# Two mixing layers of a one-core transformer block: the planner's priorities come from a written list of stage steps

## The chip, the cores and the metric

The kernel runs on one core of a Trainium2 chip. The core's engines each take their own instruction queue in order: TensorE (PE, matmuls and transposes), VectorE (DVE), ScalarE (ACT), GpSimd (POOL), and SyncE (SP), which issues the DMAs. They wait for each other by semaphores. The metric is the device time of one launch in microseconds (us); lower is better. The kernel before takes 1844.59 us, the median of three runs (1842.2 to 1846.6).

## The reference, cut to what matters

A block with two layers (DEPTH = 2) runs over 512 latent tokens and 256 context tokens of width 1024, in float32. Each layer is a mixing sublayer followed by an MLP; in the second layer the context is only read, so it has no outputs there. The mixing sublayer splits one projection of the input into four groups:

```
def mixing_sublayer(h_ctx, h_lat, pos, ctx_out, w_in, w_out, ...):
    (a, cq, ckv, kpe, q, k, v, rq, rk, rv, gf, gb) = split_cols(h @ w_in)   # context and latent
    ya = conformer_conv(a)              # a * sigmoid, 31-tap depthwise convolution, layer norm, silu, matmul
    yb = mla(cq, ckv, kpe)              # 4 heads, low-rank q and kv, rope, softmax attention
    yc = gqa(q, k, v)                   # 4 query heads, 2 kv heads, normed, rope, softmax attention
    yd = retention(rq, rk, rv, gf, gb)  # 4 heads, forward and backward, chunks of 128, gated readout
    return concatenate([ya, yb, yc, yd]) @ w_out
for layer in range(DEPTH):
    x = x + g1 * mixing(modulate(x, sh1, sc1))
    x = x + g2 * relu(modulate(x, sh2, sc2) @ w1) ** 2 @ w2     # the context too, in layer 0
return rms_norm(x, final_g)
```

`conformer_conv`, `mla` and the rest are independent of each other until the last matmul. The shifts, scales and gates come from small matmuls of the conditioning vectors with `w_mod`.

## The kernel before, in words

Most matmuls are done in a split form: a float32 operand becomes a high and a low part (`split`: a cast on DVE or ACT, then a subtraction on DVE or POOL), and `mm3` issues three matmuls per product. So each weight tile that arrives by DMA costs work on DVE, ACT or POOL before PE can use it, and so does each intermediate result.

The kernel's Python code does not issue instructions directly. Each call on an engine is recorded (`Plan.record`) with its data dependencies, its place in the record as its priority, and the engines that may do it; copies, splits and elementwise products may often go to one of two or three. `Plan.schedule` then replays the record with a cost table: whenever an engine is free it takes the available operation of lowest priority number, and the order found this way is issued on each engine. The order is thus fixed at build time; at run time nothing is reordered. All of it is issued from one helper line (L645), so rows of the trace carry that line and must be told apart by their tiles and shapes: taps read `cvw`, gains of the grouped-query attention are `gg`, PSUM tiles are `b` and `pp`, and everything else in SBUF is `m`. `Plan` also keeps a model of what DVE and POOL may not do at the same time (`_port`) and of ACT's function tables (a switch to another of `Exp`, `Silu`, `Sigmoid` is charged).

In `mixing` every stage is a generator, and `go(k, n)` advances stage `k` by up to `n` steps, which is when its operations are recorded. The stages are:

- `um`, `ug`, `ur`: projections for the MLA, the grouped-query and the retention group, on PE, one token tile per step; `a`: the convolution's input with its sigmoid gate; `gates`: the retention gates, with silu.
- `mla`, `gqa`: norms, rope and splits of the projected queries and keys, mostly on DVE, ACT and POOL; one token pair per step.
- `taps`: the convolution, 31 steps of two DVE instructions (one per channel half), 62 in all, each 783 columns wide in layer 0 and 512 in layer 1.
- `ln`: layer norm, silu and the pointwise matmul behind the convolution, one token pair per step; needs all taps.
- `u`: attention units, 24 in layer 0 and 16 in layer 1 (the first half MLA, the second half grouped-query). A unit is scores on PE, a minimum on DVE, exp on ACT, a scaling, transposes on PE, splits, a second matmul.
- `rin`, `ret`, `read`: retention set-up, its four heads, and its readout.
- `todo`: in layer 0 six pieces of modulation for later layers.

`out_proj` follows; its matmuls read the four groups in the order convolution, MLA, grouped-query, retention. The order of the steps comes from `order_of(l, nu)`, built from the tables `o0`, `o1`, `Q` and `TP`. Written out, it is this:

```
0: um mla a taps ug gqa ur todo:0 u:1 gates ln u:1 (x10) todo:1 u:1 (x3) todo:4 todo:5 u:1 u:1 todo:2
   rin todo:3 then (u:1 ret:1) x7, u:1, u ret read
1: um mla a taps ug gqa ur u:1 ln gates u:1 (x10) rin then (u:1 ret:1) x5, u ret read
```

A name without a number means all steps that are left, `u:1` means one.

Of the kernel before, what the change touches and what calls it, by code (L numbers as in the profile page):

```python
# [20 lines left out]
MC = 184  # L21
F = (0, 0)
R = (15, 3)
Q = (1, 1)
EARLY = 0
XO = 0
XL = 0
# [4 lines left out]
RSV = 88  # L32
TL = 0
TM = (0, 0, 0)
TP = (7, 20, 25, 26, 23, 23)
REL = 160.0
LONG = 300
FB = 100
# [6 lines left out]
nraw = 3  # L45
nmd = 2
nw = 10
o0 = (1, 0, 0, 9)
o1 = (1, 1, 0, 6)
J = (0, 7)  # L50
D_ = (3, 3)
NCUT = 2

DM = 1024
DFF = 4096
# [613 lines left out]
        return self.cx[hl][j]  # L669


def order_of(l, nu):

    g, x, ln, r = (o0, o1)[l][:4]
    seq = [(k, 1000) for k in ("um", "mla", "a", "taps", "ug", "gqa", "ur")] + [("u", g)]
    if x:
        seq += [("ln", 1000), ("gates", 1000)]
        at = -1
    else:
        seq += [("gates", 1000)]  # L680
        at = max(ln, g)
    if at == g:
        seq.append(("ln", 1000))
    for i in range(g, nu):
        seq.append(("u", 1))
        if i + 1 == at:
            seq.append(("ln", 1000))
        if i == nu - r:
            seq.append(("rin", 1))
        if i > nu - r and Q[l] and (i - nu + r) % Q[l] == 0:  # L690
            seq.append(("ret", 1))
    seq += [(k, 1000) for k in ("u", "ret", "read")]
    if l == 0:
        for j in sorted(range(6), key=lambda j: (-TP[j], -j)):
            seq.insert(min(TP[j], len(seq) - 2), ("todo", j))
    return seq


@with_exitstack
def block_kernel(ctx: ExitStack, tc: tile.TileContext, x, c, cx, c_ctx, w_mod, b_mod, w_in, w_out,  # L700
# [37 lines left out]
    def psG(shape=(128, 512), nm="psG"):  # L738
        return plan.tile(ph, "g", shape, F32, nm)
# [157 lines left out]
    def acc_cols(l, i, conds):  # L897
        accs = mod_acc(l, i, conds)
        for cond in conds:
            for n in range(2):  # L900
                p = psT((128, 4, 128))
                for ft in range(4):
                    a = (n * 4 + ft) * 128
                    T.transpose(p[:, ft], accs[cond][:, a:a + 128], ident)
                V.tensor_reduce(out=modc[l][:, MI[i], cond, n * 4:n * 4 + 4], in_=p, axis=AX.X, op=ALU.add)
            if i in (1, 4):
                G.tensor_scalar(out=modc[l][:, MI[i], cond], in0=modc[l][:, MI[i], cond], scalar1=1.0, scalar2=1.0,
                                op0=ALU.add, op1=ALU.mult)

    def acc_gate(l, i, conds, res):  # L910
        accs = mod_acc(l, i, conds)
        for cond in conds:
            res[cond] = wkt([128, DM], nm="gate")
            ah, al = (wkt([128, DM], F32R, nm="mhl") for _ in range(2))
            split(ah, al, accs[cond])
            for n in range(2):
                p = psT()
                for k, a in enumerate((al, ah)):
                    T.matmul(p, lhsT=ones.bitcast(F32R), rhs=a[:, n * 512:(n + 1) * 512], start=k == 0, stop=k == 1)
                VS.copy(out=res[cond][:, n * 512:(n + 1) * 512], in_=p)  # L920
# [87 lines left out]
    def mixing(l, ht, yt, todo, late=None):  # L1008
# [153 lines left out]
        um, ug, ur, vg, gates, mq, mk, mvv = {}, {}, {}, {}, {}, {}, {}, {}  # L1162
# [192 lines left out]
        units = []  # L1355
# [235 lines left out]
        def s_read():  # L1591
            for pr in opairs:
# [18 lines left out]
                for kk in range(2):  # L1611
                    for i in range(2):
# [5 lines left out]
                                        gates=s_gates, ln=s_ln, u=s_units, ret=s_ret, read=s_read).items()}  # L1618

        def go(k, n=1000):  # L1620
            if k == "rin":
                return ret_in()
            if k == "todo":
                plan.lag = TL
                todo[n]()
                plan.lag = 0
                return
            for _ in range(n):
                if next(gens[k], self_) is self_:
                    break  # L1630

        self_ = object()
        for k, n in order_of(l, len(units)):
            go(k, n)


# [17 lines left out]
    def mlp(l, ht, tiles, xs, gate, segs, then=None):  # L1654
        NCH = DFF // 512

        def first(ch):
            hid = []
            for f in range(4):
# [3 lines left out]
                for s in segs:  # L1663
                    n = (512, 256)[s]
                    o = psG(nm="h")
                    cut = (0, 256, 512) if l == DEPTH - 1 and ch == 0 and f < NCUT else (0, n)
                    for a, b in zip(cut, cut[1:]):
# [85 lines left out]
    def later(i, n):  # L1753
# [7 lines left out]
        else:  # L1761
            mod_cols(0, i, n * 512, 512, (mod_rows, mod_rows32)[how])
    
    mixing(0, ht, yt, [lambda i=i, n=n: later(i, n) for i in (3, 4, 2) for n in range(2)],
           begin)
    xt = {t: load_x(t) for t in CTX + LAT}
    out_proj(0, yt, CTX + LAT, xt, gate)
    ht = ActT(bigt, True)
    for pr in PAIRS:
# [4 lines left out]
    todo = [lambda: acc_cols(1, 0, (0, 1)), lambda: acc_cols(1, 1, (0, 1)), lambda: acc_cols(1, 3, (0,)),  # L1774
            lambda: acc_cols(1, 4, (0,)), lambda: acc_gate(1, 2, (0,), gate1)]
# [7 lines left out]
    xt = {t: xt[t] for t in LAT}  # L1783
    yt = ActT(bigt, False)
    mixing(1, ht, yt, [])
    out_proj(1, yt, LAT, xt, gate1)
    ht = ActT(bigt, False)
# [115 lines left out]
```

## Time and profile before

| what | value |
|---|---|
| runs of the kernel before | 1844.59, 1846.6, 1842.2 us; median 1844.59 |
| the profiled execution | 1847.59 us, span 1845.9 us |
| PE busy | 1706.8 us, 92% |
| DVE busy | 1355.0 us, 73% |
| ACT busy | 684.3 us, 37% |
| POOL busy | 394.6 us, 21% |
| PE's granted clock, mean | 0.958 of full speed |

The profiled execution lasts 1847.59 us, 1.7 us more than its span, and 3.0 us more than the median of the runs. Busy shares are means over very different stages: the MLPs are matmuls in a row, while in the mixing layers (33 to 543 us and 1102 to 1476 us) PE, DVE and ACT hand small pieces to each other. A clock of 1.00 in a row is PE's 2.4 GHz, 0.50 is 1.2 GHz, and a value between is a mean over a stretch that had both.

### The profile page before, as it was taken

To read this page: it belongs to the slowest core of one execution; us is meant where nothing else is said; L and a number is where in the kernel's file an instruction comes from. 1 tells how busy PE (TensorE), PEld (TensorE's weight loads), DVE (VectorE), ACT (ScalarE), POOL (GpSimd) and SP (SyncE) were. 2 spreads that over 40 slices of the span, in tenths; PEclk is the share of its full clock that TensorE was granted. 3 is DMA by queue.
4 is the path that set the end of the run, shared out by engine and by line. 5 is a ranking of instruction groups with operands and counts; after the bars stand their busy time and mean duration, and the time that the engine had idled before them with its cause. 6 is when DMAs were issued, how large, how long until landed. Compare 5 with 4: busy or idle time off the path is not lost. (4 is left out here: it accounts for less than half of the span.)

```text
span 1845.9 us, 23213 instructions
## 1 busy us (share of the span) xinstructions
PE 1706.8 (92%) x8587; PEld 1403.2 (76%) x8587; DVE 1355.0 (73%) x2309; ACT 684.3 (37%) x1257; POOL 394.6 (21%) x358
## 2 busy tenths in 40 slices
PE   6995789989999999999999999959897989999998
PEld 4784568656788877888888889748765878888886
DVE  6889448888896788676765577974988776666665
ACT  5522027977443112111211135213997342222222
POOL 3318013651510010100100021120433421000001
PEclk9998799989999999999999999969997999999999
DMA  9220031534241434424421212110121533333331
GB/s 304 67 75 12 0 97 49 173 111 133 69 138 46 137 99 130 133 88 146 158 70 47 86 36 75 47 52 12 34 60 61 167 95 100 110 96 92 103 91 58
DMA packets 140641, 168.67 MB, mean 91 GB/s; under 512 B 7658, under 2 KB 93274, under 8 KB 140528
## 3 DMA queue, kind: packets, MB, share of 16 engines
q1 hardware_dynamic: 140528, 167.20, 29.5%
q8 instruction: 67, 1.10, 0.2%
q14 instruction: 46, 0.38, 0.1%
HBM read 161.14 MB, written 2.10 MB: 88 GB/s over the span
## 5 line engine op out<-in xcount | busy, mean ns | idle before, releaser
L645 PE MATMUL b<-m,m 128*128 128x512 f32 (+5 forms) x6452 | 1366.8, 370 | 49.6 <-DVE m L645 40.7
L645 PEld LDWEIGHTS b<-m,m 128*128 128x128 f32 (+2 forms) x6452 | 1123.2, 191 | 263.4 <-DVE m L645 39.4
L645 DVE TENSOR_TENSOR m<-m,m 128x512 fp32r<-128x512 f32 (+8 forms) x665 | 548.9, 844 | 138.0 <-PE b L645 79.9
L645 ACT CAST m<-m 128x1024 fp32r<-128x1024 f32 (+6 forms) x354 | 278.8, 808 | 666.2 <-PE b L645 462.8
L645 POOL TENSOR_TENSOR m<-m,m 128x1024 fp32r<-128x1024 f32 (+11 forms) x158 | 274.7, 1750 | 1087.7 <-ACT m L645 571.4
L645 DVE TENSOR_TENSOR m<-b,m 128x512 f32<-128x512 f32 (+12 forms) x346 | 208.6, 611 | 124.3 <-PE b L645 108.6
L645 PE MATMUL pp<-m,m 128*128 128x512 f32 (+6 forms) x848 | 206.0, 369 | 18.9 <-DVE m L645 9.7
L645 PEld LDWEIGHTS pp<-m,m 128*128 128x128 f32 (+2 forms) x848 | 148.1, 197 | 56.0 <-ACT m L645 15.8
L645 PE MATMUL b<-ident,m 128*128 128x128 f32 (+4 forms) x730 | 111.2, 280 | 27.5 <-DVE m L645 24.0
L645 ACT COPY m<-b 128x512 f32<-128x512 f32 (+7 forms) x176 | 82.8, 491 | 126.6 <-PE b L645 120.4
L645 DVE TENSOR_TENSOR m<-m 128x256 f32<-128x256 f32 (+1 forms) x104 | 63.4, 611 | 82.9 <-ACT m L645 82.4
L645 PEld LDWEIGHTS b<-ident,m 128*128 128x128 f32 (+4 forms) x730 | 84.7, 141 | 48.7 <-DVE m L645 28.2
L645 DVE SCALAR_TENSOR_TENSOR m<-m,sf,m 128x1024 f32<-128x1024 f32 x80 | 102.9, 1298 | 24.3 <-DMA m<-in_w_mod_dram 24.2
L645 DVE CAST m<-m 128x512 fp32r<-128x512 f32 (+4 forms) x163 | 77.8, 481 | 56.3 <-PE pp L645 31.7
L645 ACT ACTIVATE m<-b 128x512 f32<-128x512 f32 (+1 forms) x115 | 60.6, 529 | 149.0 <-PE b L645 140.6
L645 DVE SCALAR_TENSOR_TENSOR m<-m,cvw,m 128x783 f32<-128x783 f32 (+1 forms) x120 | 100.7, 887 | 0.6
L645 DVE TENSOR_REDUCE ty<-pp 128x1 f32<-128x768 f32 (+1 forms) x66 | 60.8, 932 | 9.2 <-PE pp L645 8.6
L645 ACT ACTIVATE m<-m 128x1024 f32<-128x1024 f32 (+4 forms) x65 | 42.0, 650 | 52.5 <-DVE m L645 42.9
L645 ACT ACTIVATE m<-pp,ty 128x768 f32<-128x768 f32 (+1 forms) x66 | 58.5, 888 | 4.4 <-PE b L645 3.0
L645 POOL TENSOR_TENSOR ty<-ty,mhalf 128x1 f32<-128x1 f32 (+4 forms) x47 | 57.3, 1225 | 2.3
L645 PE MATMUL pp<-ident,m 128*128 128x128 f32 (+3 forms) x252 | 41.6, 287 | 13.4 <-ACT m L645 7.5
L645 POOL TENSOR_SCALAR ty<-ty 128x2 f32<-128x2 f32 (+4 forms) x43 | 16.3, 380 | 166.3 <-ACT m L645 107.3
(112 smaller groups left out, 669.4 us busy)
## 6 DMA issues: line engine op xcount, KB each, us to landing
m<-in_mlp_w_dram SPq DMA_DIRECT2D x128, 512.0 KB
m<-in_w_mod_dram SPq DMA_DIRECT2D x96, 512.0 KB
m<-in_w_in_dram SPq DMA_DIRECT2D x32, 512.0 KB
m<-in_w_out_dram SPq DMA_DIRECT2D x16, 512.0 KB
m<-in_x_dram SPq DMA_DIRECT2D x8, 512.0 KB
m<-in_dist_dram SPq DMA_DIRECT2D x16, 256.0 KB
m<-in_w_in_dram SPq DMA_DIRECT2D x8, 416.0 KB
m<-m SPq DMA_DIRECT2D x24, 96.0 KB
```

The costliest lines, as they stand in the source:

```text
L645: op.fn(*[f(a) for a in op.args], **{k: f(a) for k, a in op.kw.items()})
```

## The change

`order_of` and its tables are replaced by a list per layer, read from left to right; a name with `:n` advances that stage by `n` steps, without it by all that are left. What each stage computes is not touched, and neither are the planner's rules.

```diff
-o0 = (1, 0, 0, 9)
-o1 = (1, 1, 0, 6)
+ORDER = (
+    "um mla ug gqa a ur taps:2 u:1 todo:0 gates u:2 taps:2 u:1 taps:4 u:1 taps:2 todo:1 u:2 taps:2 u:1 "
+    "taps:2 u:2 todo:4 todo:5 taps:2 todo:2 taps:2 todo:3 u:1 taps:2 u:1 taps:2 u:1 taps:2 u:1 taps:2 u:2 "
+    "taps:2 rin taps:2 u:1 taps ret:1 u:1 ln:2 ret:1 u:1 ret:1 u:1 ln ret u read ",
+    "um mla ug gqa a ur:2 u:1 taps:2 ur:2 u:1 ur taps:4 u:1 taps:2 u:1 taps:2 u:2 gates taps:2 rin ret:1 "
+    "u:3 taps:4 u:1 taps:2 u:2 ret:1 u:1 taps:4 u:1 ret:1 taps:2 u:1 taps:2 u:1 taps:2 ret u taps ln read ",
+)
...
-def order_of(l, nu):
...
+def order_of(l):
+    for w in ORDER[l].split():
+        k, _, n = w.partition(":")
+        yield k, int(n or 1000)
...
-        for k, n in order_of(l, len(units)):
+        for k, n in order_of(l):
             go(k, n)
```

In both layers `taps` leaves its place ahead of `ug` and `gqa` and is cut into pieces of two or four steps; `ug` and `gqa` come before `a`; `ln` goes from before the attention units to among the last ones in layer 0 and behind all of them in layer 1; in layer 1 `gates` moves behind the sixth unit.

**VectorE, layer 0, where the convolution runs.** Tiles: `m_3622` and `m_3628` are the convolution's inputs, `cvw` its weights; `ty` and `gg` belong to `gqa`; a 128x1024 TENSOR_TENSOR is the low part of a weight tile. Before, these rows follow 36 taps in a row:

```order
L645 SCALAR_TENSOR_TENSOR m_4837<-m_3628,cvw_163,m_4837 128x783
L645 TENSOR_REDUCE ty_3566<-m_4861 128x6 x2
L645 TENSOR_REDUCE ty_3565<-m_4929 128x6
L645 TENSOR_REDUCE ty_3565<-m_5001 128x6
L645 TENSOR_REDUCE ty_3569<-m_5001 128x6
L645 TENSOR_REDUCE ty_3569<-m_5040 128x6
L645 TENSOR_TENSOR m_5061<-b_3587,m_5011 96x512
L645 TENSOR_TENSOR m_5044<-b_3585,m_5044 96x256
L645 TENSOR_TENSOR m_5044<-b_3588,m_5044 96x256
L645 SCALAR_TENSOR_TENSOR m_4837<-m_3628,cvw_163,m_4837 128x783
L645 TENSOR_TENSOR m_4856<-m_4856,ty_3568 128x384
L645 SCALAR_TENSOR_TENSOR m_4837<-m_3628,cvw_163,m_4837 128x783
```

Now all of `gqa` stands ahead of the first tap, and the taps begin between the last two products of `a`:

```order
L650 TENSOR_SCALAR m_5020<-m_3622,cvw_163,pcol_166 128x783
L650 CAST m_5026<-m_4993 128x1024
L650 SCALAR_TENSOR_TENSOR m_5020<-m_3622,cvw_163,m_5020 128x783 x8
L650 TENSOR_TENSOR m_3628<-b_3586,m_4898 128x512
L650 SCALAR_TENSOR_TENSOR m_5020<-m_3622,cvw_163,m_5020 128x783 x2
L650 TENSOR_TENSOR m_5111<-m_4993,m_5026 128x1024
L650 SCALAR_TENSOR_TENSOR m_5020<-m_3622,cvw_163,m_5020 128x783
L650 TENSOR_TENSOR m_3628<-b_3587,m_4898 128x256
L650 SCALAR_TENSOR_TENSOR m_5020<-m_3622,cvw_163,m_5020 128x783 x19
L650 TENSOR_SCALAR m_5289<-m_3628,cvw_163,pcol_166 128x783
L650 SCALAR_TENSOR_TENSOR m_5289<-m_3628,cvw_163,m_5289 128x783
L650 TENSOR_TENSOR m_5302<-m_5022,m_5099 128x1024
```

The low parts of the weights of `ur` (`m_5111` is one) stand before or between the first twelve taps instead of behind all of `taps` and `gqa`; a run of 21 taps follows, and 58 of the 62 stand ahead of the last row of `gates`.

**ScalarE, layer 0, the silu of `ln`.** `pcol` marks the silu of `ln`, `pp` and `ty` an exp of an attention unit, `lgam` an exp of retention. Before, one table load serves the silu of `gates` and `ln` together:

```order
L645 CAST m_5413<-b_3585 128x512
L645 ACT_TABLE_LOAD
L645 ACTIVATE m_4929<-b_3588,pcol_166 128x256 x2
L645 CAST m_5448<-m_4929 128x512
L645 CAST m_5459<-m_5430 128x1024
L645 CAST m_5044<-b_3588 96x256
L645 CAST m_5477<-m_5445 128x1024
L645 CAST m_5491<-m_5465 128x1024
L645 ACTIVATE m_5522<-b_3587 128x512
```

Now each token pair's silu stands among exps, between two loads:

```order
L650 ACTIVATE m_6999<-m_6999,lgam 128x512 x2
L650 ACT_TABLE_LOAD
L650 ACTIVATE m_6765<-b_3587,pcol_166 128x256 x2
L650 ACT_TABLE_LOAD
L650 ACTIVATE m_7086,ty_3565<-pp_7030,ty_3582 128x768
L650 CAST m_7104<-b_3585 128x512
```

This pattern stands three times in layer 0; the whole program has 19 table loads instead of 10.

**GpSimd, layer 0, beside the taps.** Before, these rows of `gqa` (`m_4865`, low parts of the values) stand beside the taps, behind a weight of `ug`:

```order
L645 TENSOR_TENSOR m_4699<-m_4512,m_4658 128x1024
L645 TENSOR_TENSOR m_4865<-m_4856,m_4865 128x2x64 x2
L645 TENSOR_TENSOR m_4865<-m_4925,m_4865 128x2x64
L645 TENSOR_SCALAR ty_3567<-ty_3566 128x12
L645 TENSOR_TENSOR m_4865<-m_4925,m_4865 128x2x64
```

Now they stand before `a`'s weights, and beside the taps stands `m_5135`, the low part of the fourth and last weight piece of `ur`:

```order
L650 TENSOR_TENSOR m_4760<-m_4746,m_4760 128x2x64
L650 TENSOR_TENSOR ty_3573<-ty_3572,mhalf 128x12
L650 TENSOR_TENSOR m_4967<-m_4848,m_4875 128x1024
L650 TENSOR_TENSOR m_5135<-m_5006,m_5035 128x1024
L650 TENSOR_TENSOR m_5645<-m_5588,m_5613 128x1024
```

PE reads `m_5135` in the 19th matmul of `ur`; the row after it belongs to `todo:1` and stands behind nearly all taps.

## Rows read from the trace of the kernel before

**Rows 1.** The page's forty slices of the span: TensorE's busy share in tenths.
```profile
PE   6995789989999999999999999959897989999998
```

**Rows 2.** By stretch: us, PE, PEld, DVE, ACT, POOL busy (x), clock, DMA.
```profile
161.90:204.80 42.90, 9.04 (x28) 7.16 (x28) 40.88 (x117) 5.52 (x13) 21.58 (x18) 0.56 0.05 12
204.80:285.00 80.20, 74.53 (x338) 58.74 (x337) 23.21 (x33) 17.11 (x27) 4.63 (x5) 0.98 0.18 56
285.00:477.00 192.00, 180.57 (x1029) 127.95 (x1028) 168.23 (x349) 158.73 (x332) 89.90 (x76) 0.95 0.39 120
477.00:543.00 66.00, 65.93 (x302) 54.33 (x301) 58.38 (x77) 16.78 (x25) 18.75 (x20) 1.00 0.30 88
1195.60:1228.80 33.20, 10.53 (x33) 8.26 (x34) 32.15 (x111) 5.92 (x11) 13.80 (x18) 0.54 0.06 15
1228.80:1285.00 56.20, 56.20 (x276) 48.08 (x275) 17.39 (x25) 14.54 (x23) 0.00 (x0) 1.00 0.14 44
1285.00:1434.00 149.00, 125.77 (x722) 98.30 (x721) 134.06 (x273) 128.47 (x263) 56.33 (x52) 0.92 0.18 57
1434.00:1476.00 42.00, 42.00 (x192) 34.75 (x191) 31.78 (x43) 12.80 (x18) 19.52 (x16) 1.00 0.50 152
```

**Rows 3.** Timeline of PE, layer 0: start, us, operation, [idle before, released by].
```profile
169.10 1.62 PE L645 MATMUL b<-m 96*128 96x256 f32 x6 [7.20 <-DVE m L645]
...
185.27 1.33 PE L645 MATMUL b<-ident,m 128*128 128x128 f32 x5 [14.34 <-DVE m L645]
...
199.35 2.90 PE L645 MATMUL b<-m,m 128*128 128x512 f32 x6 [12.32 <-DVE m L645]
```

**Rows 4.** Waits of PE, 1194 to 1230 us: us in total, times, longest.
```profile
PE pp L645 <- ACT m L645: 10.3, 2, 5.4
PE b L645 <- DVE m L645: 8.7, 2, 7.9
PE pp L645 <- DVE m L645: 3.7, 1, 3.7
```

**Rows 5.** By stretch, VectorE's taps alone (`cvw`): us, busy (x), clock, DMA.
```profile
101.00:161.90 60.90, 45.93 (x47) 1.00 0.12 38
161.90:204.80 42.90, 15.70 (x16) 0.56 0.05 12
1148.00:1195.60 47.60, 36.22 (x52) 1.00 0.18 51
1195.60:1228.80 33.20, 8.11 (x12) 0.54 0.06 15
```

**Rows 6.** VectorE's groups by form, 161.9 to 199.4 us: busy us, mean ns.
```profile
L645 DVE TENSOR_TENSOR m<-m,r 128x32 f32<-128x32 f32 x48 | 5.5, 182 | 0.0
...
L645 DVE TENSOR_TENSOR m<-m,gg 128x128 f32<-128x128 f32 x6 | 1.7, 284 | 0.0
```

**Rows 7.** VectorE's groups by form, 1195.6 to 1228.8 us.
```profile
L645 DVE TENSOR_TENSOR m<-m,r 128x32 f32<-128x32 f32 x48 | 5.4, 181 | 0.0
...
L645 DVE TENSOR_TENSOR m<-m,ty 128x128 f32<-128x128 f32 x1 | 0.3, 282 | 0.0
```

**Rows 8.** Table loads of ScalarE, whole span, from the groups.
```profile
L645 ACT ACT_TABLE_LOAD x10 | 12.8, 1283 | 11.3 <-DVE ty L645 8.2 <-DMA crow<-in_c_ctx_dram 2.6 <-DVE m L645 0.3
```

**Rows 9.** Timeline, layer 1, a token pair of `ln` among `gates`.
```profile
1257.42 1.04 PE L645 MATMUL b<-ident,m 128*128 128x128 f32 x8
...
1261.93 3.06 PE L645 MATMUL b<-m,m 128*128 128x256 f32 x24
...
1264.20 0.69 DVE L645 TENSOR_TENSOR m<-b,m 128x512 fp32r<-128x512 f32 x1 [0.59 <-ACT m L645]
```

**Rows 10.** Timeline of POOL, layer 0, beside the taps and just behind them.
```profile
135.28 31.12 POOL L645 TENSOR_TENSOR m<-m,m 128x128 fp32r<-128x128 f32 x3 [20.18 <-ACT m L645]
...
166.78 0.45 POOL L645 TENSOR_TENSOR m<-m,m 128x128 fp32r<-128x128 f32 x1
```

**Rows 11.** Timeline of DVE, the same stretch.
```profile
131.17 34.10 DVE L645 SCALAR_TENSOR_TENSOR m<-m,cvw,m 128x783 f32<-128x783 f32 x36
```

More of the change, by code (lines that the diff above doesn't have):

```diff
@@ L23 @@
 R = (15, 3)
-Q = (1, 1)
 EARLY = 0
@@ L34 @@
 TM = (0, 0, 0)
-TP = (7, 20, 25, 26, 23, 23)
 REL = 160.0
@@ L669, in pair @@
         return self.cx[hl][j]
-def order_of(l, nu):
[L674 to L696, printed above, removed]
+def order_of(l):
+    for w in ORDER[l].split():
+        k, _, n = w.partition(":")
+        yield k, int(n or 1000)
 @with_exitstack
```

## The prediction

> **What bounds the kernel now.** I read the page's slices first, then the busy time by stretch, then TensorE's timeline and waits where it idles, and last the groups of VectorE there. The slices show TensorE at 9 or 8 tenths in most slices; lowest, but for the start, are the fourth (138 to 185 us, 5; the fifth has 7) and the 27th (1200 to 1246 us, 5), one in each mixing layer [rows 1]. By stretch the first is 161.9 to 204.8 us, where TensorE is busy 9.04 of 42.90 us and VectorE 40.88; the second is 1195.6 to 1228.8 us, with 10.53 of 33.20 us against 32.15 [rows 2]. In layer 0 three waits, 7.20, 14.34 and 12.32 us, make the idle time, each ended by VectorE [rows 3]. In layer 1 there are 22.7 us of waits, ended by VectorE and, through exps that waited for VectorE's minima, by ScalarE [rows 4]. What VectorE does there is the rest of the taps and then the grouped-query preparation, and only behind these come the low parts of the weights that TensorE needs for `ur`. So the bound of both places is the order of VectorE's queue. Right behind them the roles turn round: in 204.8 to 285 us TensorE runs `ur` and `gates` with VectorE busy 23.21 of 80.20 us, and in 1228.8 to 1285 us with 17.39 of 56.20 [rows 2]. Then come the attention stretches (285 to 477 and 1285 to 1434 us), where VectorE is busy 87.6% (168.23 of 192) and 90.0% (134.06 of 149), ScalarE 83% and 86%, and TensorE 94% and 84%. The MLPs are full and are left alone by the change.
>
> **The change, part by part.**
>
> *The two stalls go.* The first way to price them is from TensorE. The idle time is 42.90 - 9.04 = 33.9 us and 33.20 - 10.53 = 22.7 us. The work left in these stretches ran mostly at the lower of the clock's two levels (mean 0.56 and 0.54 of 2.4 GHz [rows 2], after waits of 7 to 14 us), so about half of its 9.0 and 10.5 us goes too: 4.5 and 5.2. That makes 38.4 and 27.9, together 66.3 us.
>
> *The taps need another cover.* The second way asks whether VectorE can hold what is moved. From the end of the projections up to the end of `out_proj` (161.9 to 543 us, 381.1 us long) it is busy 40.88 + 23.21 + 168.23 + 58.38 = 290.7 us, 76% [rows 2]. In the new order the 47 taps (45.9 us [rows 5]) that now run before 161.9 come behind it, except for the 12 that stand beside the last products of `a` (12 x 0.98 = 11.7). In return the grouped-query rows leave: seven groups in a row, from the rope's 5.5 us to the 1.7 us of the last, in all 20.1 us [rows 6]; they now stand beside `ug` and `a`. That gives 290.7 + 45.9 - 11.7 - 20.1 = 304.8 us. In layer 1, 1195.6 to 1476 us is 280.4 us long with 32.15 + 17.39 + 134.06 + 31.78 = 215.4 us of VectorE; 52 taps of 36.2 us come in [rows 5], less 8 beside `a` (5.6), and nine groups of grouped-query work, 5.4 us to 0.3, in all 17.4 us, go out [rows 7]: 228.6 us. If VectorE runs these stretches as full as it runs attention today, they take 304.8 / 0.876 = 347.9 and 228.6 / 0.900 = 254.0 us: 33.2 and 26.4 us less, together 59.6. The two ways bracket the same gain from TensorE's side and from VectorE's; I take the middle, 63.0 us. The cover in layer 0 is good: all but four taps stand ahead of the last row of `gates`, beside matmuls that left VectorE 57 us free, and 46 taps beyond the 12 need 45. In layer 1 only `ur` covers them; the later ones stand among the attention units, and `gates`, which moves in there too, is matmul work in which VectorE can catch up.
>
> *The table loads.* 19 instead of 10, at 1.283 us each [rows 8]: 9 x 1.283 = 11.5 us of ScalarE. Most of the new ones stand in attention, where ScalarE is busy 83 to 86% [rows 2] and an exp that comes late delays transposes on TensorE. The cost lies between 0 and 11.5 us; I take half, 5.8, since ScalarE is neither idle there nor the bound. In a sentence that the rest does without: the Trainium skill (ScalarE: Activation LUTs, "What ACT_TABLE_LOAD costs") puts a drain of about 1.38 us beside each load, which would make it 24 us and the half 12; the row has 1.283 us for the load, and none here shows the drain apart.
>
> *`ln` at the end.* In layer 1 the last pair's transposes, silu and matmul now stand directly before `out_proj`, whose first matmuls read just that result. Such a pair takes from 1257.42 to 1264.89, 7.5 us, of which TensorE works 1.04 + 3.06 [rows 9]; `gates` covers the rest today. Behind the last unit only the readout's transposes remain as cover, so the bounds are 0 and 3.4 us; I take 3.4. In layer 0 retention heads follow, and I cost it at nothing; without that cover it would be another 3.4.
>
> *Everything else.* `ug` ahead of `a` gives `mla` and `gqa` about the same matmuls to hide under as today, in another order; nothing. DMAs of weights move with their stages; no wait of TensorE in the stalls is ended by a DMA [rows 3, 4], so nothing there.
>
> Sum: 63.0 - 5.8 - 3.4 = 53.8 us off the profiled execution's 1847.6, that is 1793.8; it lies 3.0 us above the median of the runs, so 1790.8. I predict 1791 us.
>
> **Rivals.**
>
> *A. The POOL wait.* In layer 0 a POOL subtraction of only 128x128 elements stood for some 30 us beside 36 taps in a row (three of them 31.12 us [rows 10], the run of taps from 131.17, 34.10 us long [rows 11]), and the same form took 0.45 us once the taps had ended. Now the low part of the last weight piece of `ur`, a POOL row, stands at the head of a run of 21 taps. If it has not got through when that run starts, TensorE stops at the 19th matmul of `ur` until the run ends: 21 x 0.98 = 20.6 us less 18 matmuls of about 0.22, some 16.6 us, and the time is 1807. For it: that row. Against it: a product that VectorE reads from PSUM and must wait for TensorE stands before the run, which leaves POOL an opening. The Trainium skill gives the reason (SBUF — State Buffer, "Who interferes with whom": a VectorE instruction with two inputs in SBUF excludes a GpSimd one that reads SBUF, for its whole length); the trace agrees with it as far as these rows go, and by the rule alone POOL would get its turn between two taps, with the time left at 1791.
>
> *B. Attention pays most of it back.* If VectorE can only be kept busy 84% in these stretches, between today's mean and today's attention, they take 304.8 / 0.84 = 362.9 and 228.6 / 0.84 = 272.1 us, a gain of 18.2 + 8.3 = 26.5, less 9.2 of loads and `ln`: 1844.6 - 17.3 = 1827. For it: small pieces of attention wait for each other on three engines, and taps of 0.7 to 1 us now stand between them in layer 1.
>
> *C. More than the stalls.* In layer 1's attention TensorE idles 149 - 125.77 = 23.2 us [rows 2]. If the interleaved `gates` and `ur` (240 matmuls) fill half of it, and loads and `ln` cost nothing, the gain is 66.3 + 11.6 = 77.9: 1767. Against it: VectorE would then be busy 304.8 of 342.7 us in layer 0 (89%) and 228.6 of 240.9 in layer 1 (95%), the second fuller than any long stretch of [rows 2].
>
> *D. VectorE becomes the bound, and it gets slower.* The place is the same two stretches. Before, VectorE was full for 76.3 and 76.8% of them; now it has 304.8 and 228.6 us to do, and at its old shares these take 399.5 and 297.6 us, 18.4 and 17.2 more than today; with the loads' 11.5 the time is 1892. It decides at 304.8 / 381.1 = 80% and 228.6 / 280.4 = 81.5%: below that fullness the layers get longer. For it: dependences set the share. Against it: the low share came from `ur` and `gates` with nothing for VectorE to do, and there it gets work.
>
> *E. That the change doesn't do what it says* is excluded by the order: the taps do stand elsewhere.
>
> **How the numbers follow.** My forecast, from 1780 to 1803 around 1791: 0.50. A: 0.13. B: 0.17. C: 0.14. D, with any milder form of it: 0.04; no difference 0.02. The range reaches down to C, 1767, and up to 1825, most of the way to B. Within 0.2% (3.7 us, about what a measurement of this kernel can tell from no change) I leave 0.02, slower 0.04, faster 0.94.
>
> **What would show it.** Right: no wait of TensorE over 5 us between `um` and `out_proj` in either layer, its clock at 1.00 through `ur`; one tap on VectorE beside every four or five matmuls of `ur` and `gates` in layer 0; VectorE 85 to 90% busy from there to `out_proj`; 19 table loads; a gap of some 3 us before `out_proj` in layer 1. Wrong: a POOL row of 10 us or more beside the taps with TensorE waiting (A); waits of 1 to 3 us that add up to over 60 us in attention (B, D); the MLPs changed in length.

## The result, and the profile after

The changed kernel takes 1778.93 us (median of four runs, 1775.38 to 1779.61) against 1843.39 us (1838.34 to 1846.6): a ratio of 0.9649, 95% interval 0.9623 to 0.9675. The forecast was 1791 us with a range of 1767 to 1825, so the sign and the range hold; the forecast's own stretch, 1780 to 1803, is missed by 1 us at its lower end. The profiled execution takes 1779.39 us, 68.2 less than that of before; predicted were 53.8.

The page's slices: TensorE's busy share in tenths, then its granted clock. Beside [rows 1], the two fives are gone.

```profile
PE   6999999899999999999999999999987999999998
...
PEclk9999999999999999999999998999999999999999
```

The same stretches as in [rows 2], in the kernel after (columns as there). The first four rows are layer 0, the fifth is their sum; then three rows of layer 1 and their sum.

```profile
160.30:203.00 42.70, 39.41 (x179) 30.44 (x178) 37.73 (x40) 9.77 (x19) 2.89 (x1) 1.00 0.23 67
203.00:236.00 33.00, 33.00 (x148) 27.09 (x147) 31.65 (x36) 7.98 (x13) 0.00 (x0) 1.00 0.21 70
236.00:411.00 175.00, 159.37 (x930) 113.64 (x930) 158.17 (x328) 150.22 (x314) 68.27 (x74) 0.98 0.38 116
411.00:500.00 89.00, 85.41 (x433) 70.79 (x432) 79.23 (x114) 38.07 (x68) 32.30 (x32) 1.00 0.29 87
160.30:500.00 339.70, 317.18 (x1686) 241.96 (x1685) 306.78 (x515) 206.03 (x410) 103.46 (x107) 0.99 0.32 98
1162.00:1198.00 36.00, 36.00 (x187) 31.74 (x186) 35.17 (x59) 14.60 (x25) 0.62 (x1) 1.00 0.11 36
1198.00:1356.00 158.00, 137.42 (x776) 104.62 (x775) 142.27 (x276) 133.11 (x269) 55.87 (x56) 1.00 0.17 50
1356.00:1411.00 55.00, 52.57 (x247) 44.29 (x246) 44.55 (x57) 19.89 (x30) 21.11 (x16) 0.95 0.50 162
1162.00:1411.00 249.00, 225.99 (x1207) 180.66 (x1206) 221.99 (x390) 167.60 (x322) 77.59 (x73) 0.99 0.23 73
```

The two sums of the kernel before, from the same view:

```profile
161.90:543.00 381.10, 330.07 (x1689) 248.18 (x1689) 290.70 (x574) 198.15 (x394) 134.86 (x119) 0.92 0.29 89
1195.60:1476.00 280.40, 234.50 (x1216) 189.39 (x1217) 215.38 (x447) 161.73 (x314) 89.64 (x85) 0.90 0.21 64
```

From the end of the projections to the end of `out_proj`, layer 0 is 41.4 us shorter and layer 1 31.4 us. TensorE has nearly the same matmuls in both (1689 and 1686, 1216 and 1207). Where it was busy 9.04 of 42.90 us it is busy 39.41 of 42.70, and VectorE is nearly full beside it. Two parts make the gain: idle time of TensorE falls from 51.0 to 22.5 us and from 45.9 to 23.0, together 51.4 us; and its busy time falls by 12.9 and 8.5 us, together 21.4, at a mean clock of 0.99 in place of 0.92 and 0.90. Outside of these stretches 4.6 us are given back: the projections change by -1.6 and +5.4, the MLPs by +4.0 and -3.0 us, what stands behind the last MLP by -0.2.

The waits of TensorE, 126 to 500 us, then 1133 to 1411 us: sum, times, longest.

```profile
PE b L650 <- DVE m L650: 11.8, 15, 2.3
PE pp L650 <- ACT m L650: 6.5, 8, 1.4
```

```profile
PE b L650 <- DVE m L650: 11.6, 15, 2.7
PE pp L650 <- ACT m L650: 6.5, 9, 1.4
PE b L650 <- ACT m L650: 3.8, 9, 1.1
```

In place of [rows 3, 4], with waits of up to 14 us, many short ones are left; none is over 2.7 us. The taps, which answer to [rows 5], stand beside `ur` and what follows it (columns as there; two stretches of layer 0, one of layer 1):

```profile
160.30:203.00 42.70, 28.04 (x26) 1.00 0.23 67
203.00:236.00 33.00, 22.65 (x22) 1.00 0.21 70
1162.00:1198.00 36.00, 26.33 (x39) 1.00 0.11 36
```

The grouped-query rows have left that place: the gains (`gg`), two of the groups of [rows 6], stand beside `ug` and `a` now.

```profile
101.00:160.30 59.30, 3.77 (x12) 1.00 0.19 58
160.30:203.00 42.70, 0.00 (x0) 1.00 0.23 67
```

The table loads, which answer to [rows 8]:

```profile
L650 ACT ACT_TABLE_LOAD x19 | 24.4, 1283 | 4.5 <-DMA crow<-in_c_ctx_dram 2.6 <-DVE ty L650 1.6
```

### The profile page after: what moved, and what is told of

Read it like the earlier page. It is cut to its first block, busy times and chain, and to the rows that moved or that the text cites. A ratio compares the mean times of both kernels' runs of the same rounds, so it can differ in the third digit from the quotient of the medians.

```text
span 1777.7 us, 23252 instructions
## 1 busy us (share of the span) xinstructions
PE 1687.8 (95%) x8587; PEld 1391.8 (78%) x8587; DVE 1358.9 (76%) x2305; ACT 700.6 (39%) x1278; POOL 349.4 (20%) x350
## 5 line engine op out<-in xcount | busy, mean ns | idle before, releaser
L650 PE MATMUL b<-m,m 128*128 128x512 f32 (+4 forms) x6450 | 1361.1, 369 | 27.8 <-DVE m L650 16.8
L650 PEld LDWEIGHTS b<-m,m 128*128 128x128 f32 (+1 forms) x6450 | 1120.7, 190 | 243.9 <-DVE m L650 29.7
L650 DVE TENSOR_TENSOR m<-m,m 128x512 fp32r<-128x512 f32 (+9 forms) x669 | 554.0, 848 | 104.8 <-PE b L650 80.5
L650 POOL TENSOR_TENSOR m<-m,m 128x1024 fp32r<-128x1024 f32 (+11 forms) x158 | 236.6, 1507 | 984.4 <-ACT m L650 489.9
L650 DVE TENSOR_TENSOR m<-b,m 128x512 f32<-128x512 f32 (+10 forms) x344 | 208.2, 614 | 114.6 <-PE b L650 104.5
L650 PE MATMUL pp<-m,m 128*128 128x256 f32 (+8 forms) x860 | 195.4, 357 | 12.3 <-ACT m L650 9.3
L650 PEld LDWEIGHTS pp<-m,m 128*128 128x128 f32 (+2 forms) x860 | 142.1, 191 | 44.1 <-ACT m L650 18.5
L650 PE MATMUL b<-ident,m 128*128 128x128 f32 (+4 forms) x711 | 107.5, 279 | 19.2 <-DVE m L650 14.7
L650 ACT COPY m<-b 128x512 f32<-128x512 f32 (+6 forms) x182 | 81.0, 476 | 105.7 <-PE b L650 101.1
L650 DVE SCALAR_TENSOR_TENSOR m<-m,cvw,m 128x783 f32<-128x783 f32 (+1 forms) x120 | 105.8, 904 | 1.9
L650 POOL TENSOR_TENSOR ty<-ty,mhalf 128x1 f32<-128x1 f32 (+4 forms) x47 | 55.9, 1194 | 2.3
L650 POOL TENSOR_SCALAR ty<-ty 128x2 f32<-128x2 f32 (+4 forms) x43 | 15.4, 357 | 183.3 <-ACT m L650 129.0
L650 ACT CAST m<-b 128x512 fp32r<-128x512 f32 (+6 forms) x86 | 40.8, 491 | 26.3 <-PE b L650 25.2
```

The lines of the kernel that those rows point to most:

```text
L650: op.fn(*[f(a) for a in op.args], **{k: f(a) for k, a in op.kw.items()})
```

## The experiments

Two theories to begin with. *Queue*: what counts is that the taps leave VectorE's queue ahead of `ur`'s low parts. *Pieces*: it is as much that they are cut up and spread as cover. To place a difference, I counted TensorE's 8587 matmuls, the same number in all kernels, and read when matmul 2440 (end of layer 0's mixing in the kernel after), 5235 (end of its MLP) and 6958 (end of layer 1's mixing) begin. All stretches in us, from one profiled execution each:

```
kernel                       mixing 0   MLP 0   mixing 1   MLP 1 and end   span
before                          542.6   553.3      380.1           369.8   1845.9
after                           500.0   557.0      354.0           366.7   1777.7
new list in layer 0 alone       503.4   555.4      380.3           372.7   1811.8
new list in layer 1 alone       540.8   555.9      353.1           366.5   1816.3
old lists, taps behind ur       523.1   556.1      361.7           371.9   1812.7
new lists, taps uncut           506.8   554.5      357.0           366.3   1784.6
new lists, a first              498.1   555.5      356.6           372.1   1782.3
old, values on VectorE          530.1   551.0      360.5           374.7   1816.2
old, values and ur on VectorE   542.8   555.9      382.1           371.5   1852.3
new, no silu behind ln          501.7   557.4      351.7           366.4   1777.3
new, ln earlier in layer 1      500.5   554.3      350.8           372.2   1777.8
new, ln in one go               515.4   554.8      353.8           367.1   1791.0
new, ur's low parts on VectorE  506.5   557.6      344.6           367.1   1775.8
new, values on VectorE          507.4   556.2      352.5           367.0   1783.1
```

These columns are coarse, and not only because each is one execution. The first 110 matmuls of layer 1's mixing are the same in all fourteen kernels, in the same order and behind the same wait of 1.5 us. They take 22.7 or 22.8 us at a mean granted clock of 0.70 in eleven profiles, 21.2 at 0.76 in one (new lists, `a` first), and 16.7 at 1.00 in two (old, values on VectorE; new, `ur`'s low parts on VectorE). The kernel after, then the second of these two:

```profile
1057.00:1079.80 22.80, 21.26 (x112) 20.10 (x112) 15.41 (x30) 11.47 (x25) 9.54 (x11) 0.70 0.17 47
1064.10:1080.80 16.70, 14.97 (x112) 14.08 (x111) 15.29 (x30) 11.32 (x25) 9.93 (x11) 1.00 0.12 33
```

So 6 us of a difference can be the clock alone. Three kernels whose TensorE runs the whole mixing of layer 1 in the very order of the kernel after (new list in layer 1 alone; `ln` in one go; `ur`'s low parts on VectorE) have 353.1, 353.8 and 344.6 us there, for 354.0.

**One layer at a time.** The old list is kept in the other layer.

> The new list for layer 0, the old order for layer 1. By the queue theory (each layer's gain is its own stall of TensorE, ended by VectorE's order, less what comes back in attention) layer 0 gives what its stretch lost between the two traces, about 39 us: 1804 to 1807 us, with layer 1's 22.7 us of waits still there. If instead the gain sits in what one layer hands to the next (buffers, prefetched weights), the two halves do not add up: more than 8 us off that.

> The old order for layer 0, the new list for layer 1. By the queue theory about 26 us off: 1816 to 1820 us, with layer 0's three waits of 7, 14 and 12 us unchanged. If the halves do not add up (the sum of both gains differs from 64.5 us by more than 8), something passes between the layers.

Measured: 1813.02 us, ratio 0.9802 [0.9762, 0.9842], and 1813.46 us, 0.9819 [0.9796, 0.9842]. In the table layer 0's list takes 39.2 us off its mixing stretch and layer 1's takes 27.0 off its own; both lists together 42.6 and 26.1. By the table the layers are independent, to about 3 us. By the whole time the two lists give 35.0 and 34.5 us, together 69.5 for the 64.5 of both at once, within the 8 us that was allowed for; the first kernel came out 6 us above the range expected of it, the second 3 us below its own.

**The taps moved in one block, the rest of the old lists kept.**

```diff
-um mla a taps ug gqa ur ...
+um mla a ug gqa ur taps ...
```

> The old list in both layers with one word moved: taps in one piece behind ur instead of behind a; gqa stays behind ug, ln before attention, table loads nearly as few (12). By the queue theory, where only the place of the taps behind the grouped-query work and ur's weights counts, most of the gain is here: 1780 to 1797 us. If cutting the taps into pieces among attention units is what gives the gain, TensorE starves behind ur instead, for up to the 62 x 0.98 us of taps less ur's 36 us, 25 us in layer 0 and some 10 us in layer 1: 1810 to 1825 us.

**The new lists, the taps in one piece behind `ur`.**

```diff
-um mla ug gqa a ur taps:2 u:1 todo:0 gates ...      (layer 0; the same way in layer 1)
+um mla ug gqa a ur taps u:1 todo:0 gates ...
```

> The new lists with the taps uncut, in one piece right behind ur, all else as in the changed kernel. By the queue theory within 8 us of the changed kernel's 1779, since most taps stood beside ur and gates there already. If the pieces matter, a stall of TensorE behind ur of 10 to 25 us in layer 0 and some 10 us in layer 1: 1795 to 1815 us.

Measured: 1811.47 us, ratio 0.9801 [0.978, 0.9823], and 1791.34 us, 0.9697 [0.9671, 0.9723]. Neither theory holds alone: the first time lies where *pieces* had it, the second between the two. In the first kernel the stall has only moved. TensorE's timeline, then VectorE's, layer 0:

```profile
215.77 0.47 PE L647 MATMUL pp<-ident,m 128*128 128x128 f32 x1 [16.14 <-DVE m L647]
```

```profile
174.04 42.62 DVE L647 SCALAR_TENSOR_TENSOR m<-m,cvw,m 128x783 f32<-128x783 f32 x45
```

45 taps stand in one run of 42.62 us, `ur` is done before it ends, and TensorE then waits 16.14 us for the last tap but one of this run, which the transposes of `ln` read; the low parts of the next weights come only behind the run, at 216.55 us. In the second kernel the grouped-query rows are done beside `a`, the taps begin at 147.06 us, and although the list has them in one piece, the planner issues at most 17 in a row, with low parts of weights between the runs. No such wait is left: the longest is 2.7 us in layer 0 and 4.2 in layer 1. Its first tap and its longest run on VectorE:

```profile
147.06 0.68 DVE L647 TENSOR_SCALAR m<-m,cvw,pcol 128x783 f32<-128x783 f32 x1
...
165.53 18.15 DVE L647 SCALAR_TENSOR_TENSOR m<-m,cvw,m 128x783 f32<-128x783 f32 x17
```

**The swap of `ug gqa` and `a` undone, the pieces kept.**

```diff
-um mla ug gqa a ur ...
+um mla a ug gqa ur ...
```

> The new lists, but with `a` ahead of `ug gqa` again, so that the grouped-query preparation stands beside `ur` and not beside `a`. My prediction priced this swap at nothing: by it the time stays at 1779, within 4 us. The rival, drawn from the run with the taps moved in one block (20 us slower than the uncut new lists, with VectorE's grouped-query rows beside `ur`): the swap is a part of the gain, since in `ur` VectorE then has the grouped-query rows, the taps and the weights' low parts at once; by it the time is 1789 to 1799 and TensorE waits 6 us or more once behind or within `ur`.

Measured: 1787.81 us, ratio 0.9697 [0.9674, 0.972], which is 9 us over the kernel after. The table says where they are not: mixing takes 498.1 + 356.6 = 854.7 us against 500.0 + 354.0 = 854.0, and TensorE's longest wait in layer 0 is 2.1 us. The end, from the last MLP's first matmuls on, takes 5.4 us longer (below); the profile lies 3.8 us under the median, and where the rest of the 9 us stands is open. With the two kernels above this makes a square of mixing time: taps in a block and `a` first 523.1 + 361.7 = 884.8 us (that kernel also keeps the old places of `ln`, `gates` and `todo`), block with the swap 863.8, pieces without the swap 854.7, both 854.0. The pieces bring 30.1 us without the swap and 9.8 with it. The swap brings nothing beside the pieces; without them it brings 21.0 us, or less, since the old places in the first corner, of `ln` above all, may have a part in that, which no run separates.

**Is it VectorE's queue, or POOL?** In [rows 10] POOL was held up for 31 us beside the taps. So in the kernel before I took its subtractions away from it:

```diff
-split(vg[pr][:, i, :, 0], vg[pr][:, i, :, 1], v4[:, i])
+VS.copy(out=vg[pr][:, i, :, 0], in_=v4[:, i])
+V.tensor_tensor(out=vg[pr][:, i, :, 1], in0=v4[:, i], in1=..., op=ALU.subtract)
```

> The kernel before, in its own order, but the low parts of the grouped-query values are taken on VectorE and not on POOL, where three of them stood for 31 us beside the taps. If the order of VectorE's queue makes the stall (the reason in my prediction), the time stays at 1844 within 6 us, and TensorE's waits of 7, 14 and 12 us in layer 0 stay. If it is POOL that is starved beside the taps, and TensorE's late start comes from there, the waits of layer 0 shrink to under 15 us in sum and the time falls by 10 to 20 us, to 1824 to 1834.

Measured: 1824.48 us, ratio 0.9895 [0.9867, 0.9924], at the near end of where the POOL theory had it. But the planner, with POOL free, had also given POOL two of the low parts of `ur`'s weights. The stretch of the stall, and POOL's timeline:

```profile
161.90:204.80 42.90, 27.08 (x100) 21.34 (x99) 41.94 (x116) 6.87 (x15) 18.24 (x12) 0.80 0.08 25
```

```profile
164.54 3.07 POOL L647 TENSOR_TENSOR m<-m,m 128x1024 fp32r<-128x1024 f32 x1 [49.31 <-DVE m L647]
...
174.53 3.25 POOL L647 TENSOR_TENSOR m<-m,m 128x1024 fp32r<-128x1024 f32 x1
```

TensorE is busy 27.08 us there instead of 9.04, since it gets part of `ur` early; 15.8 us of waits are left. (The table shows more for layer 1, 19.6 us, but 6.1 of these are the 110 matmuls at the full clock.) So a second kernel keeps the values on VectorE and holds `ur`'s low parts there too:

```diff
 def split(hi, lo, src, lov=False):
-    (V if on_psum(src) else VG).tensor_tensor(out=lo, ...)
+    (V if lov or on_psum(src) else VG).tensor_tensor(out=lo, ...)
-yield from group(ur, 1440, 1952, (128, 512))
+yield from group(ur, 1440, 1952, (128, 512), lov=True)
```

> The run before on this (grouped-query values' low parts on VectorE, 1824) also let POOL take two of the low parts of `ur`'s weights, so it changed two things. Here the values' low parts stay on VectorE and the low parts of `ur`'s weights are held on VectorE too, where the kernel before has them. If the 20 us came from the place of `ur`'s low parts (behind taps and grouped-query rows in VectorE's queue, as the prediction has it), the stall is back: TensorE's waits in 161 to 205 us sum to 28 us or more and the time is 1838 to 1848. If they came from the starved POOL subtractions of the values, the time stays at 1820 to 1829.

Measured: 1848.57 us, ratio 1.0012 [0.9997, 1.0026]. The stall is back without any POOL row held up. The same stretch, and TensorE's waits in it:

```profile
161.90:204.80 42.90, 10.79 (x33) 8.56 (x34) 39.43 (x118) 3.24 (x8) 14.75 (x15) 0.52 0.05 12
```

```profile
168.66 1.62 PE L647 MATMUL b<-m 96*128 96x256 f32 x6 [9.06 <-DVE m L647]
...
181.78 1.33 PE L647 MATMUL b<-ident,m 128*128 128x128 f32 x5 [11.29 <-DVE m L647]
...
197.60 2.90 PE L647 MATMUL b<-m,m 128*128 128x512 f32 x6 [14.06 <-DVE m L647]
```

34.4 us of waits, as in [rows 3]. What stalls TensorE is that `ur`'s low parts stand in VectorE's queue behind taps and grouped-query rows: the two kernels differ in the engine of these low parts alone. Letting two of them be made earlier, on another engine, took about half of the stall away; the new order takes it all.

**The table loads.**

```diff
-S.activation(out=z[:, ch], in_=p[:, ch], func=AF.Silu, ...)
+S.activation(out=z[:, ch], in_=p[:, ch], func=AF.Identity, ...)
```

> The new kernel with the silu behind `ln` left out (the identity in its place, so the output isn't the reference's): table loads fall from 19 to 12 and the activations stay. It prices the loads. The prediction charged 11.5 us of loads at half, 5.8 us for nine of them: by that the seven loads cost 4.5 us and the time is 1774 to 1775. If ScalarE's slack hides them, it stays at 1779 within 2 us; if each is paid in full (1.28 us), it is 1770.

Measured: 1778.33 us, ratio 0.9648 [0.9625, 0.9671]; mixing 853.4 us against 854.0. Seven loads, 9.0 us of ScalarE, cost nothing that these runs show. The intervals, over 4 us to either side, don't exclude the 4.5 us of the prediction by themselves; in mixing, layer 0 is 1.7 us longer without the loads, and layer 1 is 3.9 us shorter in its projections, ahead of any `ln`, and 1.6 longer behind them.

**`ln` of layer 1 earlier, and `ln` of layer 0 in one go.**

```diff
-... taps:2 ret u taps ln read      (layer 1, first kernel)
+... taps ln ret u read
-... ret:1 u:1 ln:2 ret:1 u:1 ret:1 u:1 ln ret u read      (layer 0, second kernel)
+... ret:1 u:1 ret:1 u:1 ret:1 u:1 ln ret u read
```

> The new kernel with `ln` of layer 1 moved ahead of the last retention piece and the last attention unit, so that these stand behind it as cover. The prediction charged 3.4 us for `ln` at the end of layer 1: by it the time falls to 1775 or 1776, and the waits of TensorE between 1336 and 1368 us, 8.7 us in sum, halve. If the tail is only the last unit's own chain, which stays last in either order, nothing is gained: 1779 within 2 us; if `ln` now delays that chain, it is 1 to 4 us slower.

> The new kernel with `ln` of layer 0 in one go behind the retention pieces instead of in two: 17 table loads and not 19, and the pair's chain of 7.5 us stands later. If loads and `ln` are hidden (as the runs with the identity and with the earlier `ln` say), 1779 within 3 us; if two loads or the later chain are paid, 3 to 6 us less or more.

Measured: 1781.96 us, ratio 0.9668 [0.9646, 0.969], and 1788.19 us, 0.9682 [0.9662, 0.9701]. In the first, layer 1's mixing falls by 3.2 us, near the price that the prediction put on `ln` at the end. But 2.5 of these stand in matmuls 5675 to 5785, in the projections and far ahead of `ln`: the order is the same there, while the kernel after has 26.4 us with a wait of 2.66 and a mean clock of 0.94, and this one 23.9 at 1.00. For `ln` 0.7 us are left, and the front of the last MLP takes back more. TensorE's timeline there, after, then with `ln` earlier:

```profile
1413.70 0.73 PE L650 MATMUL b<-m,ones 128*128 128x512 f32 x2 [0.60 <-ACT m L650]
1415.86 5.47 PE L650 MATMUL b<-m,m 128*128 128x256 f32 x31 [1.43 <-DVE m L650]
```

```profile
1407.81 0.94 PE L647 MATMUL b<-ident,m 128*128 128x128 f32 x4 [1.51 <-DVE m L647]
...
1412.41 5.26 PE L647 MATMUL b<-m,m 128*128 128x256 f32 x26 [3.22 <-DVE m L647]
...
1424.57 11.71 PE L647 MATMUL b<-m,m 128*128 128x256 f32 x73 [1.53 <-DVE m L647]
```

2.0 us of waits became 6.3, all ended by VectorE's norm, modulation and splits ahead of the MLP. Over the table this boundary has two lengths: 366.3 to 367.1 us in seven of the kernels, 369.8 to 374.7 in the other seven, the kernel before among these. It goes with the list of layer 1: all five kernels with the old list there are among the longer ones, and of the nine with a new list only the two that change the place of `a` or of `ln` in it. So 3.1 us of the whole gain stand at this boundary, which no term of the prediction had. The second kernel has two loads less and is slower, outside of both ranges expected of it, so the loads are not what counts; its mixing in layer 0 is 15.4 us longer in a profile that is itself above its median. From 300 us to the end of that mixing some 10 us of it are busy time of TensorE, at a mean clock of 0.96 in place of 1.00. That the late chain does it was not shown.

**Two tries for a better version.** `ur`'s low parts of layer 0 held on VectorE in the new kernel, and the grouped-query values on VectorE in the new kernel (both edits as above).

> The new kernel with the low parts of `ur`'s weights of layer 0 held on VectorE, so that POOL no longer stands beside the taps there. In the new kernel's trace that contact costs a 2.32 us wait of TensorE and a tap that takes 2 us longer, while each low part of 128x1024 takes VectorE about 1 us and POOL 2.9: 0 to 3 us less by that, 1776 to 1779. If VectorE's queue is what TensorE waits for in `ur`, the one added low part delays it by about 1 us: 1779 to 1781. Over 1783 would say that more than that hangs on POOL.

> The new kernel with the grouped-query values' low parts on VectorE, the edit that was worth 20 us on the kernel before. If what it gained was the stall of layer 0, nothing is left to gain, since the new lists have no such stall: 1776 to 1783. If POOL's subtractions cost something of their own wherever they stand, it is again 8 to 20 us faster, 1759 to 1771, and would be the best version.

Measured: 1779.69 us, ratio 0.9637 [0.9621, 0.9652], and 1779.39 us, 0.964 [0.9615, 0.9666]: no difference from the kernel after that these intervals could show. In the table the first has 6.5 us more in layer 0's mixing and 9.4 less in layer 1's, where TensorE's order is untouched and 6.0 of them are the 110 matmuls at the full clock. What the edit of the values was worth before came with `ur`'s low parts and the stall, and the new lists have no stall. No run beat the kernel after by more than its interval.

## Why the prediction was right, and where its sizes were off

**The bound** was right: the order of VectorE's queue in both places. Between the two kernels with the values on VectorE the place of `ur`'s low parts alone makes 34.4 us of waits out of 15.8 in layer 0, and some 22 to 24 us of the whole time; each layer's list by itself takes its own stall away.

**The two stalls, 63.0 us, is the term that was mis-sized.** The stretches fell by 41.4 + 31.4 = 72.8 us. With 0.7 us for the `ln` tail and nothing for the loads the stalls gave some 73.5, above both of the ways that were to bracket them. The way from TensorE's side had 56.6 us of idle time and 9.7 us of low clock; measured are 51.4 and 21.4. The step that was off is thus "the work left in these stretches ran mostly at the lower of the clock's two levels": it counted the low clock inside the stalls alone. [Rows 2] showed more of it: a mean of 0.95 over 192 us and 0.92 over 149 us of attention. Read as a share at half speed (0.05 / 0.50 of 192 and 0.08 / 0.50 of 149) that is 19.2 and 23.8 us, of which up to half, 9.6 and 11.9 us, could come back; after, the long attention rows have 0.98 and 1.00. The clock's own rows in the traces agree: in the stretches from the projections to the end of `out_proj` TensorE was busy 31.0 and 28.7 us at the lower level before, 6.8 and 6.3 after; half of the difference is 12.1 and 11.2 us, for the 12.9 and 8.5 by which its busy time fell. No run held the clock apart in these stretches; what the same matmuls take at either level is seen in the 110 ahead of them (22.7 and 16.7 us). Why the attention before had so much of the lower level, and the attention after so little, is open: nothing in the prediction would have told that the change of order gives it back. The way from VectorE's side had its busy time nearly right (306.8 for 304.8, 222.0 for 228.6 us). Its share was 90.3% and not 87.6 in layer 0, and 89.2 for 90.0 in layer 1, since beside `ur` it is full, at 31.65 of 33.00 us, as no attention stretch was.

**The table loads, 5.8 us,** were the second wrong size: 19 loads stand there as predicted, and seven of them cost nothing that showed (0.6 us by the medians, inside the intervals).

**`ln` at the end of layer 1, 3.4 us,** shows as a wait of 2.43 us directly before `out_proj`, where [rows 9] had cover. As a price it was not confirmed: with `ln` earlier the stretch gains 0.7 us, and the whole time nothing.

```profile
1361.86 2.93 PE L650 MATMUL b<-m,m 128*128 128x256 f32 x12 [2.43 <-DVE m L650]
```

**"`ug` ahead of `a`: nothing"** holds beside the pieces (0.7 us of mixing; of the 9 us of the whole time 5.4 stand behind it) and might not have held without them (up to 21.0 us). The prediction took the grouped-query rows, 20.1 and 17.4 us [rows 6, 7], as the swap's gift to VectorE's balance; beside the pieces they were not needed.

**"The MLPs are left alone"** missed by little: +4.0 and -3.0 us, with the projections' +3.8 and the end's -0.2 4.6 us against the gain. The errors close: 10.5 (stalls) + 5.8 (loads) + 2.7 (`ln`) - 4.6 = 14.4 us, all that the profiled execution came in under its forecast. Loads and `ln` are read from one profile each here, so these two parts and the stalls' are good to a few us.

**The rivals.** A did not come. The POOL row got its turn in the opening that was named against it, behind VectorE's product from PSUM, and the two taps beside it took 4.10 us in place of 2.10. TensorE waited 2.32 us behind them, for 1.28 us in two waits where `ur`'s low parts were held on VectorE. In the run of 19 taps that follows no POOL row stands. Timelines of POOL, VectorE and TensorE:

```profile
160.26 2.93 POOL L650 TENSOR_TENSOR m<-m,m 128x1024 fp32r<-128x1024 f32 x1 [23.46 <-PE b L650]
```

```profile
159.33 0.68 DVE L650 TENSOR_TENSOR m<-b,m 128x512 f32<-128x512 f32 x1
159.93 4.10 DVE L650 SCALAR_TENSOR_TENSOR m<-m,cvw,m 128x783 f32<-128x783 f32 x2
...
166.37 20.28 DVE L650 SCALAR_TENSOR_TENSOR m<-m,cvw,m 128x783 f32<-128x783 f32 x19
```

```profile
165.22 30.26 PE L650 MATMUL b<-m,m 128*128 128x512 f32 x132 [2.32 <-DVE m L650]
```

B and D needed VectorE to be kept busy 84% or less of these stretches; it was 90.3 and 89.2%. C had the right side, the time being 12 us under the forecast, but not the reason: idle time fell by 51.4 us, no more than the stalls' own 56.6, so attention's gaps were not filled on balance; what came on top was busy time. Of what was to show it, two marks were off: one tap stands beside seven matmuls of `ur`, not beside four or five, and 90.3% is over the 85 to 90.

## What to carry to other kernels

Ask of each long idle time of the bounding engine which rows of the producing engine's queue stand ahead of the one it waits for; move independent work behind that row, and see that it doesn't stand there in one run. Of the two kernels with the taps in one piece in the list, the one with 45 of them in a row on VectorE had the wait moved to the end of that row (16.1 us); in the other the planner had broken the row up. Where a stretch's granted clock is below 1.00 beside such stalls, count its slow share over the whole layer and not in the stall alone. With a scheduler that replays a list, an edit in one place reorders boundaries far off by some 5 us; to judge an edit worth less than that, compare the time of its own stretch, with the granted clock beside it: the same matmuls in the same order differed by 6 us here.

## What the runs showed that was not expected

A POOL subtraction's time was very different by when it started. Three of 128x128 elements stood 31.12 us beside a run of taps [rows 10, 11], while one of eight times the size took 2.93 us when it began behind VectorE's product from PSUM, and then the taps beside it took the longer time. And a table load cost ScalarE little more than itself. ScalarE's timeline, after, a token pair of `ln` in layer 0:

```profile
352.93 1.39 ACT L650 ACTIVATE m<-m,lgam 128x512 f32<-128x512 f32 x2
354.34 1.28 ACT L650 ACT_TABLE_LOAD   x1
355.63 1.02 ACT L650 ACTIVATE m<-b,pcol 128x256 f32<-128x256 f32 x2
356.67 1.28 ACT L650 ACT_TABLE_LOAD   x1
357.96 0.90 ACT L650 ACTIVATE m<-pp,ty 128x768 f32<-128x768 f32 x1
```

From 354.32, the end of the first row, to 357.96 there are 3.64 us, of which the two loads are 2.56 and the silu 1.02: 0.06 us are left around two switches. The Trainium skill (ScalarE: Activation LUTs, "What ACT_TABLE_LOAD costs") has some 2.66 us for a switch, 1283 ns of load and a drain of some 1380; this trace agrees in the load and not in the drain.
